# Second block's mixers: GpSimd's products and weight splits moved to VectorE and ScalarE up to the output projection

## The chip, the cores and the metric

One core of a Trainium2 chip runs the whole program in one launch. Its engines are TensorE (PE in the rows; PEld is its weight load), VectorE (DVE), ScalarE (ACT), GpSimd (POOL) and SyncE (SP), which issues the weight loads. The metric is the device time of one execution in microseconds (us); lower is better.

## The reference, cut to what matters

A first block (a chunked mLSTM and a sparse attention side by side, then a mixture of 32 experts) is followed by a second block of two layers over 272 tokens (16 meta tokens and 256 of the sequence) of width 1024. The change lies in the mixers of the second block. Cut down, a layer there is:

```
proj = rms_norm(h, norm_mix_g[l]) @ w_in[l]
q, k, v, xr, gate = jnp.split(proj, splits, axis=-1)
q = apply_partial_rope(rms_norm(q, q_norm_g[l]), cos, sin)      # k alike
o_attn = rms_norm(diff_attention(q, k, v, lam), subln_g[l]) * (1.0 - lam_init)
xc = causal conv of xr, width 4;  r, i = sigmoid(xc @ w_rg + b_rg), sigmoid(xc @ w_ig + b_ig)
log_a = 8 * r * log_sigmoid(lru_L);  a = exp(log_a)
u = sqrt(max(-expm1(2 * log_a), 0)) * i * xc                    # factor 1 at t = 0
h_t = a_t * h_(t-1) + u_t
o_rec = rms_norm(h_t * gelu(gate), rec_norm_g[l])
h = h + concat(o_attn, o_rec) @ w_out[l]
h = h + (silu(g) * u) @ w_down[l],   g, u = rms_norm(h, norm_ffn_g[l]) @ w_gu[l]
```

All of it is float32.

## The kernel before, in words

**Products in three parts.** Weights stream from HBM in tiles of 128x4096. `run` walks a list of items; a weight item is a 128x1024 piece (128x512 for `w_out`), and LEAD = 4 items ahead of its use `split` (line 1446) turns it into a high half `wh` (a cast to fp32r, ScalarE, L1449) and a low half `wl = w - wh` (L1452 on VectorE, or L1454 when an engine was named, which before the change is GpSimd for some pieces). `wh` and `wl` each have a ring of LEAD + 1 = 5 buffers. An input-projection item is 24 matmuls, three for each of 8 pieces of the contraction (L339: high x high, L340: high x low activations, L341: low weights), 128x272 each, into one bank of PSUM.

**The items of a mixer** (`layer2`), in their order: X, four pieces for the recurrent input with its convolution (`conv`); four pieces of k and four of q (`qkin`), among them the steps `lru1` to `lru5` of the recurrence; then G, four pieces of the gate, and V, four pieces of v, among them `qk_norm`, the per-head steps `knorm`, `scores`, `mix`, `turn`, `value`, `oc`, `orow`, and the recurrent branch's `gelu1`, `gelu2`, `rec_sq`, `rec_c`, `rec_r`; then R, the eight pieces of the output projection on the recurrent half, and eight on the attention half.

**q and k.** For each piece ScalarE copies the product out as `z` (L1775) and squares it (L1777), VectorE multiplies it by the cosines (L1778), TensorE rotates `z` (L1790), VectorE multiplies by the sines (L1791) and adds (L1792). `z` has a ring of two buffers (tag `vin`): the third piece's `z` waits for the first piece's L1792. TensorE gathers the sums of squares in `ps_qs` (L1787). `qk_norm` then makes all reciprocal roots in one chain of small VectorE steps (L1800, L1802, three rounds of L211 to L213, and L1804), 128x48 each. TensorE broadcasts the result (`ps_rqb`, L1811, in `knorm`), which stands on its queue behind the gate's second piece G[1] and before the third.

**The recurrence.** On tiles of 128x1088: ScalarE takes logarithms and exponentials in `lru1`; VectorE does L1708 and L1709, GpSimd squares (L1711) in `lru2`; VectorE does L1715 and L1716, GpSimd two products (L1717, L1718) in `lru3`; VectorE L1723 and L1725, GpSimd a product (L1724) in `lru4`; VectorE four scans in `lru5` (L1729). In `gelu1` GpSimd does the last product (L1740). In `rec_r` VectorE scales (L1762), ScalarE makes the high halves `yhi`, GpSimd the low halves `ylo` (L1454), which the items R read.

**Order.** The lists are written out by hand, but each engine's queue is set by the framework's scheduler from them, and each engine runs its queue strictly in order. Small chains that others wait for are marked `high_priority`. `split` without a named engine puts `wl` behind `self.mark`, the last step of the last reciprocal root traced so far:

```
if eng is None and self.mark is not None:
    with self.tc.issue_after(self.mark):
        nc.vector.tensor_tensor(lo, src, hi.bitcast(F32), op=ALU.subtract)
```

Of the kernel before, what the change touches and what calls it, by code (L numbers as in the profile page):

```python
# [13 lines left out]
AF = mybir.ActivationFunctionType  # L14
ALU = mybir.AluOpType
# [179 lines left out]
class Kernel:  # L195
# [1429 lines left out]
    def layer2(self, l):  # L1625

        tc, nc, d = self.tc, self.nc, self.d
# [6 lines left out]
        def tile_(nm, shape, dt=F32, tag=None, bufs=1):  # L1634
            return B["px"].tile(shape, dt, name=f"{nm}_{l}", tag=tag or nm, bufs=bufs)

        def part(nm, k):

            key = (nm, k // 4)
            if key not in B:  # L1640
                tag = {("yhi", 0): "rr", ("yhi", 1): "ii", ("ylo", 0): "xc", ("ylo", 1): "gl"}[key]
                B[key] = tile_(f"{nm}{k // 4}", [P, 4, T2], F32R, tag)
            return B[key][:, k % 4]
# [61 lines left out]
        def lru2():  # L1705
            th, c, y, t = B["rr"], B["xc"], B["ry"], B["rt"]

            nc.vector.scalar_tensor_tensor(t, th, 1.0, c, op0=ALU.add, op1=ALU.mult)  # L1708
            nc.vector.scalar_tensor_tensor(c, t, 2.0, c, op0=ALU.subtract, op1=ALU.mult)  # L1709

            nc.gpsimd.tensor_tensor(t, y, y, op=ALU.mult)  # L1711

        def lru3():
            th, c, y, t, ii = B["rr"], B["xc"], B["ry"], B["rt"], B["ii"]
            nc.vector.scalar_tensor_tensor(t, t, -0.5, th, op0=ALU.mult, op1=ALU.mult)  # L1715
            nc.vector.scalar_tensor_tensor(y, t, 1.5, y, op0=ALU.add, op1=ALU.mult)  # L1716
            nc.gpsimd.tensor_tensor(ii, ii, c, op=ALU.mult)  # L1717
            nc.gpsimd.tensor_tensor(y, y, th, op=ALU.mult)  # L1718

        def lru4():  # L1720
            th, c, y, t, ii = B["rr"], B["xc"], B["ry"], B["rt"], B["ii"]

            nc.vector.tensor_scalar(y[:, :, 0:1], th[:, :, 0:1], 0.5, 0.5, op0=ALU.mult, op1=ALU.add)  # L1723
            nc.gpsimd.tensor_tensor(ii, ii, y, op=ALU.mult)  # L1724
            nc.vector.tensor_scalar(t, c, -2.0, -1.0, op0=ALU.mult, op1=ALU.add)  # L1725

        def lru5():
# [3 lines left out]
        def gate(n):  # L1731
            def f(po):
                nc.vector.tensor_tensor(B["gl"][:, n], po, self.rb, op=ALU.mult)
            return f

        def gelu1():
            gl, t = B["gl"], B["rt"]
            nc.scalar.activation(t, gl, AF.Square)
            nc.vector.tensor_scalar(t, t, 0.044715, 1.0, op0=ALU.mult, op1=ALU.add)
            nc.gpsimd.tensor_tensor(t, t, gl, op=ALU.mult)  # L1740

        def gelu2():
            gl, t, hr = B["gl"], B["rt"], B["ry"]
# [14 lines left out]
        def rec_r():  # L1758
            hr = B["ry"]
            r = self.col_rows(B["recr"], T2, f"rec{l}")  # L1760
            for n in range(4):
                nc.vector.scalar_tensor_tensor(hr[:, n], hr[:, n], self.col("recg", 4 * l + n), r,  # L1762
                                               op0=ALU.mult, op1=ALU.mult)
                self.split(part("yhi", 4 + n), part("ylo", 4 + n), hr[:, n], nc.gpsimd)


        def qkin(i):
# [38 lines left out]
        def knorm(i):  # L1806
            def f():
                prb = self.ps(f"ps_rqb{l}{i}")
                for j, (o, m) in enumerate(self.chunks(T2)):
                    for c in range(2):  # L1810
                        nc.tensor.matmul(prb[64 * c : 64 * c + 64, o : o + m],  # L1811
                                         B["rq"][:m, j, 2 * i + c : 2 * i + c + 1].to_broadcast([m, 64]),
                                         self.ident[:m, :m], start=True, stop=True)
                nc.vector.tensor_tensor(B["qk"][:, i], B["qk"][:, i], prb[:, :T2], op=ALU.mult)
            return f


        def vin(n):
            def f(po):
                v = tile_(f"v{n}", [P, T2], tag="vin", bufs=2)  # L1820
                nc.vector.tensor_tensor(v, po, self.rb, op=ALU.mult)
                B["v", n] = v
            return f
# [51 lines left out]
        def mix(h):  # L1875
            def f():
                e, ea, sm = B["e", h], B["ea", h], B["sm", h]
                parts = [(e, P, slice(0, T2), 0), (e, P, slice(T2, 416), 1)]
                parts += [(ea, 16, slice(0, 16), 2)] if l == 0 else []
                for ap, m, cs, q in parts:  # L1880
                    nc.vector.reciprocal(sm[:m, q], sm[:m, q])
                    nc.vector.tensor_tensor(sm[:m, q, 1:2], sm[:m, q, 1:2], self.nlam[:m, l : l + 1], op=ALU.mult)
                    nc.vector.tensor_scalar(ap[:m, 0, cs], ap[:m, 0, cs], sm[:m, q, 0:1], None, op0=ALU.mult)
                    nc.vector.scalar_tensor_tensor(ap[:m, 0, cs], ap[:m, 1, cs], sm[:m, q, 1:2], ap[:m, 0, cs],
                                                   op0=ALU.mult, op1=ALU.add)
            return f
# [33 lines left out]
        def oc(h):  # L1920
            def f():
                B["or", h] = self.col_sums(B["px"], B["osq", h][:, t0:], nq, P, f"ro{l}{h}")
            return f
# [55 lines left out]
        pool = nc.gpsimd  # L1979
# [5 lines left out]
        def inp(c, n, then, eng=None):  # L1985
            return self.lin_f(("win", l, c), n * 1024, KT, xin, self.after_rows(then), eng)[0]
# [11 lines left out]
        def out(k, part, last):  # L1998
            a = slice(4 * part, 4 * part + 4)
            return self.lin_f(("wout", l, k // 4), (k % 4) * 1024 + 512 * part, 4, lambda: tuple(x[a] for x in xmid(a)),  # L2000
                              add_mix(k, last), pool if last else None)[0]

        R = [out(k, 1, False) for k in range(KT)]
        G = [inp(1, n, gate(n), pool if n > 1 else None) for n in range(4)]
        V = [inp(4, n, vin(n), pool) for n in range(4)]
        it += [G[0], qk_norm, G[1], knorm(4), knorm(5), G[2], scores(0), knorm(6), G[3], scores(1),
               mix(0), knorm(7), gelu1, V[0], turn(0), scores(2), vtr(0), mix(1), gelu2,
               V[1], value(0), turn(1), scores(3), vtr(1), mix(2), rec_sq, V[2], oc(0), value(1), turn(2), vtr(2), mix(3), rec_c,
               V[3], orow(0), oc(1), value(2), turn(3), vtr(3), rec_r, R[0], orow(1), oc(2), value(3), R[1], R[2],
               orow(2), oc(3), R[3], R[4], orow(3)]  # L2010
        it += R[5:]
# [31 lines left out]
```

## Time and profile before

| what | value |
|---|---|
| median of 3 runs | 1934.74 us (1932.25 to 1937.94) |
| the profiled execution's own time | 1937.82 us |
| its span, first to last instruction | 1936.1 us |
| granted TensorE clock, mean over the span | 0.935 |
| busy share: PE, DVE, ACT, POOL | 90%, 42%, 29%, 14% |
| layer 0's mixer / layer 1's mixer (us from the start) | about 1190 to 1370 / 1585 to 1735 |

The profile's busy shares are averages over the whole program. The change touches two stretches of some 130 us, one in each layer, and is read from the rows of those: the busy time of each engine in slices, what TensorE waited for there, and the instructions in order of time with their durations. A row of an instruction gives its time from start to end; neighbours on VectorE overlap a little, so that from one start to the next is about 0.08 us less. The granted clock tells which of its two levels TensorE ran at: 1.00 is 2.4 GHz, 0.50 is 1.2 GHz.

### The profile page before, as it was taken

What the parts mean: (1) busy time and instruction counts of PE and PEld (TensorE: products, weight loads), DVE (VectorE), ACT (ScalarE), POOL (GpSimd) and SP (SyncE); (2) the same over time, 40 slices, a digit from 0 to 9 for tenths busy, and PEclk for the clock granted to TensorE, in tenths of its full rate; (3) what the DMA queues carried; (4) which work ended last, traced back from release to release, by engine and by line L of the source; (5) the groups of instructions that cost most, each with busy time, mean ns of one, the idle gap of its engine ahead of it and who ended that gap; (6) DMA issues with size and microseconds to landing.
All of it is one profiled execution on the core that took longest, in us unless ns stands there. A gap on an engine that the chain in (4) does not pass through costs nothing.

```text
span 1936.1 us, 34266 instructions
## 1 busy us (share of the span) xinstructions
PE 1739.4 (90%) x14551; PEld 1231.3 (64%) x14552; DVE 810.0 (42%) x1806; ACT 568.3 (29%) x1127; POOL 264.4 (14%) x259
## 2 busy tenths in 40 slices
PE   6999899866999997799999766989999998889998
PEld 3786743433544543454354334977999998789998
DVE  3573632211122222122222114587666557876653
ACT  2564511100111110011010102525544445354442
POOL 2322300000000000000000001051233103223320
PEclk8999889976999998899999878888999999889999
DMA  9658589999899999999999997220443453125441
GB/s 387 236 183 322 203 351 427 428 428 425 367 428 429 426 426 427 428 425 428 428 426 427 426 428 330 88 88 1 174 174 134 167 206 120 56 95 192 166 152 51
DMA packets 42698, 556.68 MB, mean 288 GB/s; under 512 B 4788, under 2 KB 5964, under 8 KB 8360
## 3 DMA queue, kind: packets, MB, share of 16 engines
q1 hardware_dynamic: 40368, 548.41, 69.4%
q0 software_dynamic: 1200, 4.29, 0.6%
q8 instruction: 116, 1.90, 0.4%
q10 hardware_dynamic: 968, 1.70, 0.3%
q14 instruction: 46, 0.38, 0.1%
HBM read 553.32 MB, written 1.06 MB: 286 GB/s over the span
## 4 chain that ended last, share of the span: by engine, by line
PE 56%; DMA 12%; DVE 5%; ACT 1%; issue 0%; ACTq 0%; POOL 0%; DVEq 0%; POOLq 0%
DMA we<-wexp 12%; PE ps_lin L339 9%; PE ps_lin L340 9%; PE ps_lin L341 9%; PE ps_l L1320 7%; PE ps_u L1320 6%; PE ps_d L1320 6%; PE ps_g L1286 2%; PE ps_c L1383 2%; DVE qk L1792 1%; PE ps_at L1363 1%; PE ps_rqb L1811 0%; PE ps_ri L1686 0%; PE ps_pg L1348 0%; PE nm0ss L1500 0%
## 5 line engine op out<-in xcount | busy, mean ns | idle before, releaser
L339 PE MATMUL ps_lin<-xhi,wh 128*128 128x272 f32 (+1 forms) x1024 | 301.6, 295 | 0.2 <-ACT xhi L1430 0.2
L340 PE MATMUL ps_lin<-xlo,wh 128*128 128x272 f32 (+1 forms) x1024 | 297.3, 291 | 1.0 <-DVE xlo L1431 1.0
L341 PE MATMUL ps_lin<-xhi,wl 128*128 128x272 f32 (+1 forms) x1024 | 297.4, 291 | 0.0
L1320 PE MATMUL ps_d<-we,at 128*32 128x256 f32 (+1 forms) x2048 | 223.0, 482 | 48.5 <-DMA we<-wexp 39.0
L1320 PE MATMUL ps_l<-we,xg 128*32 128x256 f32 (+1 forms) x2048 | 217.2, 461 | 29.7 <-DMA we<-wexp 29.5
L1320 PE MATMUL ps_u<-we,xg 128*32 128x256 f32 (+1 forms) x2048 | 212.4, 454 | 25.5 <-DMA we<-wexp 24.6
L339 PEld LDWEIGHTS ps_lin<-xhi,wh 128*128 128x128 f32 x1024 | 197.4, 193 | 2.8 <-DVE qk L1778 0.8
L340 PEld LDWEIGHTS ps_lin<-xlo,wh 128*128 128x128 f32 x1024 | 197.3, 193 | 1.8 <-DVE xlo L1431 1.4
L341 PEld LDWEIGHTS ps_lin<-xhi,wl 128*128 128x128 f32 x1024 | 197.3, 193 | 0.0
L1320 PEld LDWEIGHTS ps_d<-we,at 128*32 128x32 f32 (+1 forms) x2048 | 90.4, 128 | 165.0 <-issue 102.2
L1320 PEld LDWEIGHTS ps_l<-we,xg 128*32 128x32 f32 (+1 forms) x2048 | 88.6, 123 | 139.4 <-issue 97.2
L1320 PEld LDWEIGHTS ps_u<-we,xg 128*32 128x32 f32 (+1 forms) x2048 | 87.1, 121 | 128.0 <-issue 76.1
L1387 DVE TENSOR_TENSOR hT<-hT,ps_c 128x512 f32<-128x512 f32 x128 | 79.4, 681 | 151.7 <-PE ps_c L1383 151.7
L1406 POOL TENSOR_TENSOR hT<-hT,g 128x1024 f32<-128x1024 f32 x1 | 3.3, 3261 | 946.1 <-DVE ssm L1404 946.1
L1449 ACT CAST wh<-wgu 128x1024 fp32r<-128x1024 f32 x88 | 92.2, 1049 | 122.1 <-PE ps_lin L340 121.4
L1452 DVE TENSOR_TENSOR wl<-wgu,wh 128x1024 fp32r<-128x1024 f32 x88 | 108.2, 1231 | 41.6 <-ACT wh L1449 41.6
L1332 DVE TENSOR_SCALAR gl<-ps_u 128x512 f32<-128x512 f32 (+1 forms) x36 | 20.3, 572 | 217.1 <-PE ps_u L1324 217.1
L1364 ACT COPY at<-ps_at 128x512 f32<-128x512 f32 (+1 forms) x36 | 17.3, 492 | 299.9 <-PE ps_at L1363 299.1
L339 PE MATMUL ps_lin<-ahi,wh 128*128 128x272 f32 (+1 forms) x352 | 100.6, 286 | 0.0
L341 PE MATMUL ps_lin<-ahi,wl 128*128 128x272 f32 (+1 forms) x352 | 100.0, 284 | 0.0
L340 PE MATMUL ps_lin<-alo,wh 128*128 128x272 f32 (+1 forms) x352 | 99.9, 284 | 0.0
L1288 ACT ACTIVATE xg<-ps_g,modc,a2c 128x128 f32<-128x128 f32 (+1 forms) x120 | 43.8, 452 | 171.0 <-PE ps_g L1286 171.0
(677 smaller groups left out, 2920.9 us busy)
## 6 DMA issues: line engine op xcount, KB each, us to landing
we<-wexp SPq DMA_DIRECT2D x192, 2048.0 KB, 27.3
wgu<-wgu SPq DMA_DIRECT2D x22, 2048.0 KB, 7.7
win<-win SPq DMA_DIRECT2D x14, 2048.0 KB, 9.1
wada<-wada SPq DMA_DIRECT2D x12, 2048.0 KB, 7.9
wdn<-wdn SPq DMA_DIRECT2D x16, 1408.0 KB, 6.0
wout<-wout SPq DMA_DIRECT2D x6, 2048.0 KB, 7.7
wint<-wint SPq DMA_DIRECT2D x2, 2048.0 KB, 9.3
wins<-wins SPq DMA_DIRECT2D x1, 1264.0 KB, 28.1
```

The lines of the kernel that those rows point to most:

```text
L339: nc.tensor.matmul(po[:m, :nn], hi[:, a], xh[k], start=(k == 0), stop=False)
L340: nc.tensor.matmul(po[:m, :nn], hi[:, a], xl[k], start=False, stop=False)
L341: nc.tensor.matmul(po[:m, :nn], lo[:, a], xh[k], start=False, stop=(k == nk - 1))
L1286: nc.tensor.matmul(p, self.x[:, tt, k * P : k * P + P], oh[:, tt], start=(tt == 0), stop=(tt == 1))
L1288: nc.scalar.activation(xg[:, k], pg[:, (k - k0) * n : (k - k0) * n + n], AF.Identity, scale=self.a2c[:, k : k + 1], bias=self.modc2[:, k : ...
L1320: nc.tensor.matmul(dst[b][s], lhs(k, b), ws[k // 4][:, o : o + wd], start=(k == 0 and b % per == 0), stop=False)
L1332: nc.vector.tensor_scalar(gl[i], pu[i], 7.0, 0.5, op0=ALU.min, op1=ALU.mult)
L1363: nc.tensor.transpose(pt[:, c * P : c * P + P], li[i][:, c * P : c * P + P], self.ident)
L1383: nc.tensor.matmul(pc[s][:, (tt - t0) * wd : (tt - t0) * wd + wd], gt[b][rows[s], tt * P : tt * P + P], y[b // per][rows[s], (b % per) * w ...
L1387: nc.vector.tensor_tensor(a, a, pc[s].rearrange("p (a b) -> p a b", a=per), op=ALU.add)
L1449: nc.scalar.copy(hi, src)
L1452: nc.vector.tensor_tensor(lo, src, hi.bitcast(F32), op=ALU.subtract)
```

## The change

In each of the two layers, five products of 128x1088 leave GpSimd: the square L1711 goes to ScalarE (an activation), and L1717, L1718, L1724 and L1740 go to VectorE. So do the low halves `wl` of six weight pieces (G[2], G[3] and V[0] to V[3]) and the four low halves `ylo` of the recurrent branch. GpSimd keeps the low halves of the output projection's last eight pieces and its work in the feed-forward part.

```diff
--- before.py
+++ after.py
@@ -1708,20 +1708,20 @@
             nc.vector.scalar_tensor_tensor(t, th, 1.0, c, op0=ALU.add, op1=ALU.mult)
             nc.vector.scalar_tensor_tensor(c, t, 2.0, c, op0=ALU.subtract, op1=ALU.mult)
 
-            nc.gpsimd.tensor_tensor(t, y, y, op=ALU.mult)
+            nc.scalar.activation(t, y, AF.Square)
 
         def lru3():
             th, c, y, t, ii = B["rr"], B["xc"], B["ry"], B["rt"], B["ii"]
             nc.vector.scalar_tensor_tensor(t, t, -0.5, th, op0=ALU.mult, op1=ALU.mult)
             nc.vector.scalar_tensor_tensor(y, t, 1.5, y, op0=ALU.add, op1=ALU.mult)
-            nc.gpsimd.tensor_tensor(ii, ii, c, op=ALU.mult)
-            nc.gpsimd.tensor_tensor(y, y, th, op=ALU.mult)
+            nc.vector.tensor_tensor(ii, ii, c, op=ALU.mult)
+            nc.vector.tensor_tensor(y, y, th, op=ALU.mult)
 
         def lru4():
             th, c, y, t, ii = B["rr"], B["xc"], B["ry"], B["rt"], B["ii"]
 
             nc.vector.tensor_scalar(y[:, :, 0:1], th[:, :, 0:1], 0.5, 0.5, op0=ALU.mult, op1=ALU.add)
-            nc.gpsimd.tensor_tensor(ii, ii, y, op=ALU.mult)
+            nc.vector.tensor_tensor(ii, ii, y, op=ALU.mult)
             nc.vector.tensor_scalar(t, c, -2.0, -1.0, op0=ALU.mult, op1=ALU.add)
 
         def lru5():
@@ -1737,7 +1737,7 @@
             gl, t = B["gl"], B["rt"]
             nc.scalar.activation(t, gl, AF.Square)
             nc.vector.tensor_scalar(t, t, 0.044715, 1.0, op0=ALU.mult, op1=ALU.add)
-            nc.gpsimd.tensor_tensor(t, t, gl, op=ALU.mult)
+            nc.vector.tensor_tensor(t, t, gl, op=ALU.mult)
 
         def gelu2():
             gl, t, hr = B["gl"], B["rt"], B["ry"]
@@ -1761,7 +1761,7 @@
             for n in range(4):
                 nc.vector.scalar_tensor_tensor(hr[:, n], hr[:, n], self.col("recg", 4 * l + n), r,
                                                op0=ALU.mult, op1=ALU.mult)
-                self.split(part("yhi", 4 + n), part("ylo", 4 + n), hr[:, n], nc.gpsimd)
+                self.split(part("yhi", 4 + n), part("ylo", 4 + n), hr[:, n], nc.vector)
 
 
         def qkin(i):
@@ -2001,8 +2001,8 @@
                               add_mix(k, last), pool if last else None)[0]
 
         R = [out(k, 1, False) for k in range(KT)]
-        G = [inp(1, n, gate(n), pool if n > 1 else None) for n in range(4)]
-        V = [inp(4, n, vin(n), pool) for n in range(4)]
+        G = [inp(1, n, gate(n)) for n in range(4)]
+        V = [inp(4, n, vin(n)) for n in range(4)]
         it += [G[0], qk_norm, G[1], knorm(4), knorm(5), G[2], scores(0), knorm(6), G[3], scores(1),
                mix(0), knorm(7), gelu1, V[0], turn(0), scores(2), vtr(0), mix(1), gelu2,
                V[1], value(0), turn(1), scores(3), vtr(1), mix(2), rec_sq, V[2], oc(0), value(1), turn(2), vtr(2), mix(3), rec_c,
```

The scheduler places the moved work anew. On VectorE's queue in layer 0, from the sines of the first q piece on (`qk` and `z` belong to q and k, `ii`, `rt`, `ry`, `rr`, `xc` to the recurrence, `wl` are low halves of weights; the numbers tell buffers apart), this stood before:

```order
L1791 TENSOR_TENSOR z_0_11391<-ps_rot_11443,sin 128x272
L1778 SCALAR_TENSOR_TENSOR qk_0_10955<-ps_lin_11410,qgs,cos 128x272
L1792 TENSOR_TENSOR qk_0_10955<-qk_0_10955,z_0_11391 128x272
L1715 SCALAR_TENSOR_TENSOR rt_10952<-rt_10952,rr_11235 128x1088
L1716 SCALAR_TENSOR_TENSOR ry_10951<-rt_10952,ry_10951 128x1088
L1791 TENSOR_TENSOR z_0_11435<-ps_rot_11488,sin 128x272
L1725 TENSOR_SCALAR rt_10952<-xc_10953 128x1088
L1792 TENSOR_TENSOR qk_0_10955<-qk_0_10955,z_0_11435 128x272
L1778 SCALAR_TENSOR_TENSOR qk_0_10955<-ps_lin_11455,qgs,cos 128x272
L1791 TENSOR_TENSOR z_0_11480<-ps_rot_11532,sin 128x272
```

and this stands there now:

```order
L1717 TENSOR_TENSOR ii_11236<-ii_11236,xc_10953 128x1088
L1791 TENSOR_TENSOR z_0_11391<-ps_rot_11443,sin 128x272
L1715 SCALAR_TENSOR_TENSOR rt_10952<-rt_10952,rr_11235 128x1088
L1452 TENSOR_TENSOR wl_11452<-win_01_10795,wh_11451 128x1024
L1778 SCALAR_TENSOR_TENSOR qk_0_10955<-ps_lin_11410,qgs,cos 128x272
L1792 TENSOR_TENSOR qk_0_10955<-qk_0_10955,z_0_11391 128x272
L1716 SCALAR_TENSOR_TENSOR ry_10951<-rt_10952,ry_10951 128x1088
L1791 TENSOR_TENSOR z_0_11435<-ps_rot_11488,sin 128x272
L1452 TENSOR_TENSOR wl_11496<-win_01_10795,wh_11495 128x1024
L1778 SCALAR_TENSOR_TENSOR qk_0_10955<-ps_lin_11455,qgs,cos 128x272
L1718 TENSOR_TENSOR ry_10951<-ry_10951,rr_11235 128x1088
L1725 TENSOR_SCALAR rt_10952<-xc_10953 128x1088
```

The products L1717 and L1718 and two weight splits have come in between the steps of q, k and the recurrence. Further on in the same queue, the end of `qk_norm`'s chain was:

```order
L211 TENSOR_TENSOR rq_t<-rq_y 128x48
L1733 TENSOR_TENSOR gl_10954<-ps_lin_11597,rb_10895 128x272
L212 SCALAR_TENSOR_TENSOR rq_t<-rq_t,rqv_11577 128x48
L213 SCALAR_TENSOR_TENSOR rq_y<-rq_t,rq_y 128x48
L1804 TENSOR_TENSOR rq_y<-rq_y,nm0r_y 128x48
L1729 SCALAR_TENSOR_TENSOR ry_10951<-rt_10952,ii_11236 128x272 x4
```

and is now:

```order
L211 TENSOR_TENSOR rq_t<-rq_y 128x48
L212 SCALAR_TENSOR_TENSOR rq_t<-rq_t,rqv_11577 128x48
L213 SCALAR_TENSOR_TENSOR rq_y<-rq_t,rq_y 128x48
L1452 TENSOR_TENSOR wl_11594<-win_04_10797,wh_11593 128x1024
L1452 TENSOR_TENSOR wl_11640<-win_04_10797,wh_11639 128x1024
L1804 TENSOR_TENSOR rq_y<-rq_y,nm0r_y 128x48
L1814 TENSOR_TENSOR qk_0_10955<-qk_0_10955,ps_rqb_11623 128x272
```

The two weight splits, whose place is behind the marked root, stand right before the chain's last step L1804 (L1733 and the scans L1729 are no longer here). The head of that chain was:

```order
L1800 SCALAR_TENSOR_TENSOR rqv_11577<-ps_qs_11186,r_0_11187 128x48
L1802 TENSOR_SCALAR rqv_11577<-rqv_11577 128x48
L209 TENSOR_SCALAR rq_y<-rqv_11577 128x48
L211 TENSOR_TENSOR rq_t<-rq_y 128x48
L212 SCALAR_TENSOR_TENSOR rq_t<-rq_t,rqv_11577 128x48
```

and is now:

```order
L1800 SCALAR_TENSOR_TENSOR rqv_11577<-ps_qs_11186,r_0_11187 128x48
L1729 SCALAR_TENSOR_TENSOR ry_10951<-rt_10952,ii_11236 128x272 x4
L1733 TENSOR_TENSOR gl_10954<-ps_lin_11597,rb_10895 128x272
L1802 TENSOR_SCALAR rqv_11577<-rqv_11577 128x48
L209 TENSOR_SCALAR rq_y<-rqv_11577 128x48
```

The four scans of the recurrence, which stood behind L1804, now stand inside the chain, behind its first step, with the gate's product L1733. GpSimd's queue has none of the moved products and splits any more, and layer 1's queues change in the same way.

## Rows read from the trace of the kernel before

**Rows 1.** Stretches: length, busy us of PE, PEld, DVE, ACT, POOL, PEclk, DMA

```profile
1260.00:1280.00 20.00, 15.91 (x101) 15.30 (x101) 19.86 (x16) 4.47 (x7) 18.78 (x8) 0.85 0.29 106
1640.00:1660.00 20.00, 9.78 (x58) 8.58 (x58) 19.43 (x30) 2.75 (x4) 13.07 (x6) 0.73 0.30 106
```

**Rows 2.** Who waited for whom, layer 0's mixer, TensorE: total us, times, longest

```profile
PE ps_rqb L1811 <- DVE rq_y L1804: 5.4, 1, 5.4
PE ps_rot L1790 <- ACT z L1775: 5.4, 3, 4.1
```

**Rows 3.** Layer 0, VectorE in order of time: start, us, operation, [idle before]

```profile
1254.63 1.29 DVE L1708 SCALAR_TENSOR_TENSOR rt<-rr,xc 128x1088 f32<-128x1088 f32 x1 [1.49 <-ACT xc L1702]
...
1257.39 1.22 DVE L1452 TENSOR_TENSOR wl<-win,wh 128x1024 fp32r<-128x1024 f32 x1
1258.53 0.49 DVE L1778 SCALAR_TENSOR_TENSOR qk<-ps_lin,qgs,cos 128x272 f32<-128x272 f32 x1
1258.94 0.43 DVE L1791 TENSOR_TENSOR z<-ps_rot,sin 128x272 f32<-128x272 f32 x1
...
1260.69 3.60 DVE L1715 SCALAR_TENSOR_TENSOR rt<-rt,rr 128x1088 f32<-128x1088 f32 x1
1264.33 3.36 DVE L1716 SCALAR_TENSOR_TENSOR ry<-rt,ry 128x1088 f32<-128x1088 f32 x1
...
1267.96 2.55 DVE L1725 TENSOR_SCALAR rt<-xc 128x1088 f32<-128x1088 f32 x1
1270.44 2.71 DVE L1792 TENSOR_TENSOR qk<-qk,z 128x272 f32<-128x272 f32 x1
...
1281.70 0.19 DVE L209 TENSOR_SCALAR rq_y<-rqv 128x48 int32<-128x48 int32 x1
1281.93 0.21 DVE L211 TENSOR_TENSOR rq_t<-rq_y 128x48 f32<-128x48 f32 x1
...
1286.47 0.21 DVE L1804 TENSOR_TENSOR rq_y<-rq_y,nm0r_y 128x48 f32<-128x48 f32 x1
1286.60 2.56 DVE L1729 TENSOR_TENSOR_SCAN ry<-rt,ii 128x272 f32<-128x272 f32 x4
```

**Rows 4.** Order of time, layer 0, GpSimd

```profile
1260.44 2.71 POOL L1717 TENSOR_TENSOR ii<-ii,xc 128x1088 f32<-128x1088 f32 x1
1263.09 6.84 POOL L1454 TENSOR_TENSOR wl<-win,wh 128x1024 fp32r<-128x1024 f32 x2
1269.89 2.96 POOL L1718 TENSOR_TENSOR ry<-ry,rr 128x1088 f32<-128x1088 f32 x1
```

**Rows 5.** Order of time, layer 0, VectorE: two shapes with GpSimd idle

```profile
1246.09 0.72 DVE L1698 TENSOR_SCALAR rr<-rr 128x1088 f32<-128x1088 f32 x1
...
1249.73 0.44 DVE L1792 TENSOR_TENSOR qk<-qk,z 128x272 f32<-128x272 f32 x1
```

**Rows 6.** Order of time, layer 0, ScalarE: a cast behind G[1]; a square of 128x1088

```profile
1281.23 1.04 ACT L1449 CAST wh<-win 128x1024 fp32r<-128x1024 f32 x1 [6.28 <-PE ps_lin L340]
...
1301.92 1.10 ACT L1738 ACTIVATE rt<-gl 128x1088 f32<-128x1088 f32 x1
```

**Rows 7.** Who waited for whom, layer 1's mixer, TensorE

```profile
PE ps_rqb L1811 <- DVE rq_y L1804: 6.1, 1, 6.1
...
PE ps_v L1829 <- DVE v L1821: 1.4, 1, 1.4
PE ps_pt L1893 <- DVE e L1884: 1.2, 1, 1.2
```

**Rows 8.** Order of time, layer 1, VectorE: a 128x4 step of scores

```profile
1674.57 2.31 DVE L1863 SCALAR_TENSOR_TENSOR mx<-mx,rq_y 128x4 f32<-128x4 f32 x1
```

**Rows 9.** Order of time, layer 1, GpSimd: the gelu product

```profile
1674.39 2.48 POOL L1740 TENSOR_TENSOR rt<-rt,gl 128x1088 f32<-128x1088 f32 x1 [6.38 <-DVE rt L1739]
```

**Rows 10.** Busy time in the stretch behind turn(1)'s wait in layer 1

```profile
1683.80:1686.50 2.70, 2.70 (x13) 1.72 (x12) 2.31 (x6) 2.70 (x9) 0.00 (x0) 0.50 0.00 0
```

## The prediction

> **What bounds the kernel now.** I read four views, each of the two mixers alone. The busy times in stretches come first: from 1260 to 1280 us VectorE was busy for 19.86 of 20 us and GpSimd for 18.78, while TensorE had 4 us with nothing to do; layer 1 shows the same from 1640 to 1660, with TensorE busy for only 9.78 [rows 1]. The waits say for what TensorE stood still: 5.4 us in layer 0 and 6.1 us in layer 1 for the last step of `qk_norm`'s chain, L1804 [rows 2, 7], and up to 4.1 us for a `z` of q [rows 2], in a row that reads the same for layer 1; that `z` itself waits for an L1792 of VectorE, whose buffer it takes. So VectorE sets the time here; the order of time shows what it is busy with. The wide L1715 took 3.60 us and L1716 3.36 us, where L1708, the same operation on the same shape, took 1.29 us [rows 3]. L1725 took 2.55 us and its like 0.72; an L1792 took 2.71 us and another 0.44 [rows 3, 5]. The long ones have their ends in common with GpSimd: L1715 ends at 1264.29 us, one plain duration after GpSimd's L1717 (1263.15); L1725 ends 0.58 us after the second split (1269.93), the L1792 0.30 us after L1718 (1272.85) [rows 3, 4]. L1791, which reads PSUM, kept its 0.43 us. I read this as standing still: a VectorE instruction with its inputs in SBUF lets the GpSimd instruction in front of it finish, and the wait is counted as busy.
>
> The Trainium skill has this as a rule: "SBUF — State Buffer", section "SBUF: two separate sides", calls the port pair that the two engines share an exclusive lock, held for the whole instruction. The rows above agree.
>
> **The change, part by part.** *The chain up to L1804, layer 0.* In the new order VectorE has the following from the start of L1708 (1254.63) to the start of L1804, priced from start to start without GpSimd [rows 3, 5]: seven wide two-input products (L1708, L1709, L1715, L1716, and the moved L1717, L1718, L1724) at 1.21 us, 8.5; six weight splits (five of them moved) at 1.14, 6.8; four L1778 at 0.41, 1.6; four L1791, five L1792 and two L1733 at 0.35, 3.9; L1725 at 0.64; L1723 at about 0.1; four scans, which now stand inside the chain, 2.5; twelve small steps of the chain at 0.23, 2.8. The sum is 26.8 us. Before, the same stretch took 1286.47 - 1254.63 = 31.8 us, of which the like sum without the moved work and the scans is 15.0, so that 16.8 us was standing still. Removed: 16.8; added: 5.7 of splits, 3.6 of products, 2.5 of scans, 11.8 together. L1804 comes 5.0 us sooner; I take 4.8, with 0.2 for hand-overs between engines that the prices do not hold. The bounds are 0, if all of it were eaten by new waits, and 16.8, if nothing that was added stood on the path; the order puts it there, so I stay by the sum.
>
> Does anything else hold VectorE up on the way? The second of the two splits in front of L1804 needs a cast by ScalarE, which needs a buffer that TensorE frees with the end of G[1]; before, that was at 1281.23 us, and the cast took 1.04 [rows 6]. The `z` of the last q piece may now start behind an L1792 that by the prices above ends near 1269 us and not at 1273.15 [rows 3], so that TensorE's 4.1 us wait goes and G[1] ends by 1277.2; the cast is done by 1278.3, and VectorE, by the prices, comes to that split at 1280. Nothing holds it up. TensorE then waits for L1804 in one piece, at least 4 us and more if G[1] keeps the full clock. Behind a wait of 1.2 us already the clock stood at 0.50 [rows 7, 10]; it stands so behind this one, before and after, and I count no difference.
>
> *Layer 1's chain* is the same list and has the same stalls: another 4.8. Two layers: 9.6 us.
>
> *The square on ScalarE* takes about 1.0 us (its like took 1.10 [rows 6]) and delays the next `z` by that; two wide products, a split and more stand on VectorE's queue in front of that `z`'s sines, so I cost it at nothing. Without that cover it would be 1.0 us a layer.
>
> *The attention part.* VectorE gets V[3]'s split (1.14) and the gelu product L1740 (1.20) and loses GpSimd's lock: in layer 1 a step of 128x4 took 2.31 us, ending with GpSimd's L1740 [rows 8, 9], and TensorE waited for what stood behind it, 1.4 us for L1821 and 1.2 us for `e` in turn(1); then it ran 2.7 us at clock 0.50, which costs half of that [rows 7, 10]. That is 2.6 + 1.3 = 3.9 us to be had. Going down the new queue with the same prices, turn(0) is late by 0.4, turn(1) by 0.2 and turn(2) by 0.7; I keep 2.6 us. In layer 0 TensorE had no such wait; the new queue brings `e` some 0.1 to 0.7 us before TensorE comes to it, with nothing to spare, and I take 0.6 as loss. Bounds for both layers: a gain of 3.9, a loss in the second rival below.
>
> *The four `ylo`* cost VectorE 1.4 us (four at 0.35) and put the next head's root behind them; on the other side TensorE gets each sooner than from GpSimd, and the lock goes here too. I cost the exchange at 0, between +1.4 and -1.4 us a layer.
>
> *What stays:* the output projection's splits on GpSimd and their locks, the feed-forward, the first block; no DMA is issued otherwise.
>
> Sum: 9.6 + 2.6 - 0.6 = 11.6 us. The profiled execution took 1937.8 us, so it would take 1926.2; it lies 3.1 us above the median of the three runs shown, 1934.7, and against that median the time is **1923.1 us**.
>
> **The rivals.** *First, G[1] is late.* If the `z` of the last q piece still starts as late as before, TensorE ends G[1] at 1281.2 as it did; the cast (1.04) and the second split (1.14) follow, and L1804 starts at 1283.4, a gain of 3.0 us a layer. With the attention part at nothing that is 6 us: 1929. For it: VectorE's queue has no slack. Against: L1792 stands before, not behind, the splits that matter.
>
> *Second, and slower: VectorE becomes late for every head.* TensorE ran through layer 0's attention part without a wait, so each delay of `mix` or `scores` on the fuller queue is a new wait. One like turn(1)'s, 1.2 us, with the 1.3 us that the low clock took behind it [rows 7, 10], costs 2.5 us. At all eight turns of the two layers that is 20 us against the chains' 9.6: 1945. It decides from four of the eight turns on. For it: nothing to spare in my walk down the queue. Against: the lock in that part, 2.3 us in layer 1, is as long as the two instructions that take its place.
>
> *Third, the long rows are VectorE's own work.* Then nothing is given back and 11.8 us a layer is added: 1958. The rows with a plain twin speak against it. The Trainium skill, "Perfetto Trace Analysis", section "Optimizing Scalar/DVE Operations", says that moving work off a saturated VectorE, to GpSimd even, may make sense, and this change goes the other way; the same section warns that the two share a port. The rows bear out the warning, and I give the rule 3 in 100.
>
> *Fourth, more than the sum:* the chains give all of 5.0, layer 1's attention part its 3.9 with no loss in layer 0, and the `ylo` 1.4 a layer: 16.7 us, 1918.
>
> **How the numbers follow.** The forecast has 0.70, the first rival 0.13, the fourth 0.08, the second 0.06, the third 0.03. The range takes in the fourth and the first with 1 us of scatter of the median: 1916.5 to 1930.5. A measurement of this kernel can tell 0.3%, 5.8 us, from no change. The forecast, the fourth and 0.05 of the first rival lie beyond that: 0.83 faster; the other 0.08 of the first and half of the second make 0.11 the same; the rest, 0.06, is slower.
>
> **What would show it.** Right: VectorE's L1715, L1716 and L1792 at 1.3 and 0.44 us; L1804 some 27 us after L1708's start instead of 32; one wait for it of 4 to 8 us and none for `z` above 1 us; no wait at L1829 in layer 1. Wrong: long rows with GpSimd idle; the same 5 us wait for L1804 as before; waits at turn(0) to turn(3) of over 1 us with a clock of 0.50 behind them.

## The result and the profile after

The change takes 1913.9 us (median of 4, 1907.5 to 1916.6) against 1934.95 us before: 0.989 of the time, 95% interval 0.9876 to 0.9905. The gain is 21.1 us where 11.6 were forecast, and 1913.9 lies below the range.

Busy times in stretches at the same distance behind L1708 as in [rows 1] (same columns). GpSimd is at 0 in both, TensorE's idle time fell from 10.2 to 7.4 us in layer 1's stretch, and rose from 4.1 to 6.0 in layer 0's, into which most of the wait for L1804 now falls. VectorE is as full as before in layer 0 but has 7 us free in layer 1.

```profile
1252.31:1272.31 20.00, 14.02 (x107) 13.40 (x106) 19.65 (x41) 5.92 (x10) 0.00 (x0) 0.93 0.29 106
1624.85:1644.85 20.00, 12.63 (x94) 11.24 (x96) 12.88 (x32) 3.18 (x4) 0.00 (x0) 0.74 0.17 71
```

The order of time on VectorE, layer 0, answers to [rows 3, 5]:

```profile
1246.94 1.29 DVE L1708 SCALAR_TENSOR_TENSOR rt<-rr,xc 128x1088 f32<-128x1088 f32 x1 [1.49 <-ACT xc L1702]
...
1252.80 1.29 DVE L1715 SCALAR_TENSOR_TENSOR rt<-rt,rr 128x1088 f32<-128x1088 f32 x1
1254.00 1.22 DVE L1452 TENSOR_TENSOR wl<-win,wh 128x1024 fp32r<-128x1024 f32 x1
1255.13 0.50 DVE L1778 SCALAR_TENSOR_TENSOR qk<-ps_lin,qgs,cos 128x272 f32<-128x272 f32 x1
1255.54 0.43 DVE L1792 TENSOR_TENSOR qk<-qk,z 128x272 f32<-128x272 f32 x1
1255.89 1.29 DVE L1716 SCALAR_TENSOR_TENSOR ry<-rt,ry 128x1088 f32<-128x1088 f32 x1
...
1258.99 1.29 DVE L1718 TENSOR_TENSOR ry<-ry,rr 128x1088 f32<-128x1088 f32 x1
1260.19 0.72 DVE L1725 TENSOR_SCALAR rt<-xc 128x1088 f32<-128x1088 f32 x1
...
1271.17 2.35 DVE L1452 TENSOR_TENSOR wl<-win,wh 128x1024 fp32r<-128x1024 f32 x2
1273.44 0.20 DVE L1804 TENSOR_TENSOR rq_y<-rq_y,nm0r_y 128x48 f32<-128x48 f32 x1
```

L1715 and L1716 take 1.29 us (3.60 and 3.36 before), L1725 0.72 (2.55), L1792 0.44 (2.71). L1804 starts 26.50 us behind L1708; before it was 31.84. The two splits of 1271.17 stand in front of it, as the order said. ScalarE's square, and its cast behind G[1], which answers to [rows 6]:

```profile
1249.88 1.12 ACT L1711 ACTIVATE rt<-ry 128x1088 f32<-128x1088 f32 x1 [0.37 <-DVE xc L1709]
...
1266.24 1.04 ACT L1449 CAST wh<-win 128x1024 fp32r<-128x1024 f32 x1 [3.17 <-PE ps_lin L340]
```

What TensorE waited for in layer 0 (total us, times, longest), for [rows 2]:

```profile
PE ps_rqb L1811 <- DVE rq_y L1804: 7.4, 1, 7.4
PE ro03r L1476 <- DVE ro_y L213: 1.9, 1, 1.9
PE ps_rot L1790 <- ACT z L1775: 1.3, 2, 0.7
PE ps_lin L339 <- ACT yhi L1449: 1.0, 1, 1.0
PE ps_lin L340 <- DVE ylo L1454: 0.9, 1, 0.9
```

There is one wait for L1804, of 7.4 us, and none of 4 us for `z`; the sum of the two fell from 10.8 to 8.7 us. Layer 1 has the same rows, with 2.2 at the fourth root and 0.8 at `ylo`. The waits of [rows 7] at L1829 and turn(1) are gone; two short ones are new, the first at turn(2), the second at turn(0):

```profile
PE ps_pt L1893 <- DVE mx L1863: 0.4, 1, 0.4
PE ps_pt L1893 <- DVE e L1884: 0.3, 1, 0.3
```

Between marks that every trace has, the starts of TensorE's rows give the table below. "x" is the first `ps_x` of layer 0's mixer, "q" the first `ps_rqb` (L1811) of a layer, "y" its first matmul on `yhi`, "r" the broadcast of its fourth head's root (`ro03r`, `ro13r`). The traces are of before (its second one is e5, with idle memsets far behind) and of the change (the last is e6, likewise).

| stretch | before | change | forecast gain |
|---|---|---|---|
| start to x | 1196.6, 1198.1, 1191.0 | 1188.8, 1197.2, 1195.1, 1193.2 | 0 |
| x to q, layer 0 | 90.2, 89.7, 90.1 | 84.9, 84.9, 84.5, 84.8 | 4.8 |
| q to y, layer 0 | 49.4, 49.3, 49.4 | 46.6, 46.6, 46.4, 46.6 | -0.6 |
| y to r, layer 0 | 19.2, 18.8, 19.1 | 19.8, 19.9, 15.6, 15.6 | 0 |
| r to q, layer 1 | 301.7, 301.7, 301.7 | 296.4, 296.5, 296.5, 296.5 | 4.8 |
| q to y, layer 1 | 44.5, 44.4, 43.4 | 40.8, 40.8, 41.1, 41.2 | 2.6 |
| y to r, layer 1 | 18.0, 18.0, 18.0 | 18.5, 18.5, 17.0, 17.0 | 0 |
| x to last r | 523.0, 521.9, 521.8 | 507.0, 507.2, 501.0, 501.7 | 11.6 |

The chains gave 5.2 us each and layer 1's attention part 3.1. The rest was not forecast: 2.8 us in layer 0's attention part, and a stretch behind `yhi` that takes 15.6 or 19.8 us in executions of the same kernel. The mixers as a whole gain 15 or 21 us by that. The first of the four traces of the change also had the shortest first block of all 14 traces (1188.8 us, others to 1198.1), so the pair that I read first put 7.7 us into code that the change does not touch.

### The profile page after: what moved, and what is told of

It is laid out like the page before. It is cut to its first block, busy times and chain, and to the rows that moved or that the text cites. A ratio compares the mean times of both kernels' runs of the same rounds, so it can differ in the third digit from the quotient of the medians.

```text
span 1912.6 us, 34255 instructions
## 1 busy us (share of the span) xinstructions
PE 1722.9 (90%) x14551; PEld 1221.2 (64%) x14552; DVE 794.9 (42%) x1834; ACT 570.6 (30%) x1129; POOL 197.6 (10%) x229
## 4 chain that ended last, share of the span: by engine, by line
PE 57%; DMA 12%; DVE 5%; ACT 1%; issue 0%; ACTq 0%; DVEq 0%
DMA we<-wexp 12%; PE ps_lin L339 9%; PE ps_lin L340 9%; PE ps_lin L341 9%; PE ps_l L1320 7%; PE ps_u L1320 6%; PE ps_d L1320 6%; PE ps_g L1286 2%; PE ps_c L1383 2%; DVE wl L1452 1%; PE ps_at L1363 1%; PE ps_rqb L1811 0%; PE ps_ri L1686 0%; PE ps_pg L1348 0%; PE nm0ss L1500 0%
## 5 line engine op out<-in xcount | busy, mean ns | idle before, releaser
L1320 PE MATMUL ps_d<-we,at 128*32 128x256 f32 (+1 forms) x2048 | 215.4, 465 | 46.8 <-DMA we<-wexp 36.9
L1320 PE MATMUL ps_u<-we,xg 128*32 128x256 f32 (+1 forms) x2048 | 217.5, 466 | 31.5 <-DMA we<-wexp 31.5
L1364 ACT COPY at<-ps_at 128x512 f32<-128x512 f32 (+1 forms) x36 | 17.3, 492 | 302.4 <-PE ps_at L1363 301.6
```

Of the source, the lines that this page charges most:

```text
L1320: nc.tensor.matmul(dst[b][s], lhs(k, b), ws[k // 4][:, o : o + wd], start=(k == 0 and b % per == 0), stop=False)
```

## The experiments

All times are medians beside runs of before on the same chip (1933.2 to 1934.7 us), but for e9 and e10, which are one execution each; "mixers" is the last row of the table, and a "fall" is a stretch in which TensorE's granted clock is at 0.50.

**e1, e9 and e10: the change and before once more.** No edit.

> The changed kernel once more. Measured so far: 21.1 us less by the medians, 23.5 us by the two profiled spans, of which 7.7 us lie ahead of the first ps_x of layer 0's mixer (1196.6 us before, 1188.8 after), where no instruction was changed, and 16.0 us between that point and the fourth root row of layer 1's mixer (523.0 us before, 507.0 after). Theory A, the first block scatters from run to run: the mixers take 507.0 us again within 0.5, the first ps_x comes anywhere from 1187 to 1197 us, and the medians differ by 14 to 21 us. Rival B, the change makes the first block faster too (its program lies differently in memory): first ps_x at 1189 us again within 1.5, and the medians differ by 20 us or more.

Measured: 1912.5 us, 0.9877 of before (0.9861 to 0.9894). First `ps_x` at 1197.2, mixers 507.2: rival B falls, the first block scatters. But then the medians should differ by less than the 22.2 us they do; theory A's 507.0 cannot be the usual value either.

> The changed kernel, one more trace. Two of its traces have TensorE at clock 0.50 for 10.2 us behind the 1.0 us wait for yhi in both layers (mixers 507.0 and 507.2 us); the trace with the 24 memsets behind them has the same instructions and the same waits there and no low clock in layer 0, 6.8 us in layer 1 (mixers 501.7). Theory: whether the clock falls there is drawn anew in each execution, so this trace may have either, the mixers anywhere from 500 to 507.2 us, with L1804 26.5 us behind L1708 and the waits the same in any case; the first ps_x from 1188 to 1198. Rival: it is the program that decides: 507.1 us again within 0.3.

Measured: 1913.0 us, mixers 501.0, 6.2 us less than in e1, in the same kernel. The rival falls. The two traces have the same waits at `yhi` and `ylo`, TensorE's order of time in e1,

```profile
1328.75 0.39 PE L339 MATMUL ps_lin<-yhi,wh 128*128 128x272 f32 x1 [1.04 <-ACT yhi L1449]
1330.02 0.59 PE L340 MATMUL ps_lin<-ylo,wh 128*128 128x272 f32 x1 [0.88 <-DVE ylo L1454]
```

and in e9:

```profile
1326.03 0.39 PE L339 MATMUL ps_lin<-yhi,wh 128*128 128x272 f32 x1 [1.04 <-ACT yhi L1449]
1327.30 0.40 PE L340 MATMUL ps_lin<-ylo,wh 128*128 128x272 f32 x1 [0.88 <-DVE ylo L1454]
```

The second matmul takes 0.59 us in the one and 0.40 in the other. The stretches of 10.2 us from 0.55 us behind the start of `yhi`'s first matmul (columns as in [rows 1], the granted clock third from the end), e1:

```profile
1329.30:1339.50 10.20, 9.48 (x35) 8.32 (x36) 4.85 (x20) 2.39 (x6) 0.00 (x0) 0.50 0.00 0
```

and e9:

```profile
1326.58:1336.78 10.20, 9.48 (x68) 8.75 (x69) 7.84 (x29) 4.05 (x9) 0.00 (x0) 1.00 0.01 2
```

TensorE ran at 1.2 GHz in the one, behind this wait, and stayed at 2.4 GHz in the other; there it did about twice as many matmuls. The two executions ran on different chips, so the chip could be the cause. But behind x an execution takes 725.5 us in e1 and 717.9 in e9 (its time less its start to x). Four of e1's five executions took 1911.0 to 1913.2 us; with e1's figure they would have had x at 1185.5 to 1187.7 us, sooner than in any of the 14 traces, with e9's at 1193.1 to 1195.3. By this estimate most executions on e1's chip had no such fall either, or a shorter one.

The Trainium skill, "TensorE: Matmul & The Clock Gate", section "What's actually happening", says that the number of slow matmuls at a kernel's start varies between runs of one kernel. The two traces show the like for a fall in mid-kernel (35 matmuls in 10.2 us and 68).

> The kernel before, one more trace. Its two traces so far (one with the memsets at the end) have the low clock behind the 0.6 us wait for ro00r in layer 0, 13.7 and 10.2 us of it before and behind the yhi wait, and the mixers at 523.0 and 521.9 us. Theory: with a wait of 0.6 us ahead of yhi's 1.0 us the fall is there each time: 8 us or more of low clock in that place, mixers 521 to 524 us. Rival: the fall is as much a matter of chance as in the changed kernel: none or 3.4 us of it, mixers 516 to 519 us.

Measured: 1929.5 us, 13.7 us of low clock in that place again, mixers 521.8. The rival falls. In before the fall comes earlier, behind a wait of 0.6 us that I had not counted. TensorE's order of time there in its first trace, and the stretches before the fall, from it to `yhi`'s wait, and from `yhi`'s first matmul on:

```profile
1328.64 1.03 PE L1476 MATMUL ro00r<-ident,ro_y 128*128 128x128 f32 x6 [0.60 <-DVE ro_y L213]
1329.60 0.83 PE L1467 MATMUL ro01c<-ones,osq 128*128 128x1 f32 x6
...
1336.15 0.59 PE L339 MATMUL ps_lin<-yhi,wh 128*128 128x272 f32 x1 [1.04 <-ACT yhi L1449]
```

```profile
1328.10:1332.00 3.90, 3.36 (x20) 2.79 (x21) 3.23 (x15) 0.92 (x3) 0.00 (x0) 0.99 0.00 0
1332.00:1335.11 3.11, 3.11 (x15) 2.26 (x13) 1.01 (x5) 1.48 (x4) 0.00 (x0) 0.50 0.00 0
1336.15:1345.70 9.55, 9.23 (x32) 7.69 (x33) 4.67 (x18) 2.38 (x6) 3.44 (x4) 0.51 0.00 0
```

Behind the wait came the root's broadcast and six sums of one column (128x1); from 1332.0 us the clock is at 0.50, and it is still there when the `yhi` item begins, so that its matmuls run at half speed. All three traces of before show 10.2 to 13.7 us of low clock here.

**e2, e3 and e4: the parts of the change.**

```
e2   G[2], G[3], V[0..3]: inp(...) without pool; all else as before
e3   L1711 nc.scalar.activation(..., Square); L1717, L1718, L1724 nc.vector; all else as before
e4   e2 and e3 together; L1740 and ylo (L1764) stay nc.gpsimd
```

> Only the six weight splits a layer move; the recurrence's square and products, the gelu product and the ylo stay on GpSimd. From the start of L1708 to the start of L1804 it took 31.8 us before and 26.5 us after. Theory: VectorE stands still for each GpSimd instruction that it meets, 2.5 to 3 us for each of three or four products, and no longer 3.4 us for each of four to five splits, but has five splits of 1.14 us more: 31.8 - 14 + 5.7 + some 2.5 of scans = 26 to 28 us, and the whole run 8 to 13 us below before. Rival: the stall depends on the products alone (they write what VectorE reads next): then L1804 comes later than before, 36 us or more, and the run is slower than before by 8 us.

> Only the recurrence's square and three products move (L1711 to ScalarE; L1717, L1718, L1724 to VectorE); the splits, the gelu product and the ylo stay on GpSimd. Theory: the splits on GpSimd go on stopping VectorE, some 10 to 14 us before L1804, the products' stalls of 7 to 8 us go and 3.6 us of products come: 31.8 - 7.5 + 3.6 = 27 to 29 us from L1708 to L1804, and the run 4 to 10 us below before. Rival: splits and products stop VectorE only where both engines want the same tiles: then this takes all of the gain at L1804 (26.5 us) and the run is as fast as the change.

Measured: e2 0.9956 (0.994 to 0.9971), 1927.1 us, from L1708 to L1804 29.8 us; e3 0.9975 (0.9964 to 0.9986), 1930.75 us, 30.5 us in layer 0 and 29.8 in layer 1. Both rivals fall: either kind of GpSimd work stops VectorE, whether or not the tiles are shared. But the theory's size was off too: 26 to 28 and 27 to 29 us were expected to L1804, and the runs gained 7.6 and 4.0 us where 8 to 13 and 4 to 10 were expected. At L1804 in layer 0 the two halves gain 2.1 and 1.4 us, both together 5.3. The rows tell why. VectorE in e2, then GpSimd:

```profile
1258.98 2.26 DVE L1452 TENSOR_TENSOR wl<-win,wh 128x1024 fp32r<-128x1024 f32 x1
...
1261.58 2.34 DVE L1792 TENSOR_TENSOR qk<-qk,z 128x272 f32<-128x272 f32 x1
1263.85 1.28 DVE L1715 SCALAR_TENSOR_TENSOR rt<-rt,rr 128x1088 f32<-128x1088 f32 x1
...
1268.26 2.29 DVE L1725 TENSOR_SCALAR rt<-xc 128x1088 f32<-128x1088 f32 x1
```

```profile
1260.13 3.49 POOL L1717 TENSOR_TENSOR ii<-ii,xc 128x1088 f32<-128x1088 f32 x1
1266.53 3.44 POOL L1718 TENSOR_TENSOR ry<-ry,rr 128x1088 f32<-128x1088 f32 x1 [2.91 <-DVE ry L1716]
```

VectorE in e3, then GpSimd:

```profile
1261.28 3.13 DVE L1715 SCALAR_TENSOR_TENSOR rt<-rt,rr 128x1088 f32<-128x1088 f32 x1
...
1264.74 2.21 DVE L1792 TENSOR_TENSOR qk<-qk,z 128x272 f32<-128x272 f32 x1
...
1270.04 2.91 DVE L1725 TENSOR_SCALAR rt<-xc 128x1088 f32<-128x1088 f32 x1
```

```profile
1260.49 6.17 POOL L1454 TENSOR_TENSOR wl<-win,wh 128x1024 fp32r<-128x1024 f32 x2 [38.76 <-ACT wh L1449]
1268.83 3.52 POOL L1454 TENSOR_TENSOR wl<-win,wh 128x1024 fp32r<-128x1024 f32 x1 [2.18 <-ACT wh L1449]
```

In e2 a moved split takes 2.26 us and L1792 2.34 beside products that now take 3.49 and 3.44 us (2.71 and 2.96 in [rows 4]); in e3 L1715 takes 3.13 and L1725 2.91. What is left on GpSimd meets a fuller VectorE queue, and each stops the other.

> The change without its late part: the gelu product L1740 and the four ylo stay on GpSimd. Past L1804 the change gained 2.8 us in layer 0 and 3.6 us in layer 1 up to the first yhi matmul. Theory A, the clock: TensorE fell to its low level twice around the chain (behind the wait for z and behind that for L1804) and falls once now; so layer 0 keeps its 2.8 us here, and layer 1 loses at most the 2.6 us of its two waits with 1.3 us of low clock behind them: the run is 0 to 4 us slower than the change. Rival B, the lifted lock in the attention part itself: both gains go, and the run is 6 us or more slower than the change, with the same L1804.

Measured: 1917.1 us, 0.9911 (0.9893 to 0.9928), 4.6 us above e1; L1804 at 26.5; layer 0's q to y 46.7 as in the change, layer 1's 41.8, 0.8 us more. Theory A allowed 4 us at most and is missed by 0.6. Rival B falls: the gelu product and the `ylo` are not what gave layer 0 its 2.8 us. Who did: the wait for `ro00r` of 0.6 us is in all traces of before and in e3, and in none of e2, e4 and the change, and layer 0's q to y is 49.3 to 49.5 in the first group and 46.4 to 46.7 in the second. With the splits on VectorE, the last step of that root (L213) no longer stands behind an L1821 on its queue that waits for TensorE. VectorE in before,

```profile
1328.07 0.44 DVE L1821 TENSOR_TENSOR v<-ps_lin,rb 128x272 f32<-128x272 f32 x1 [0.26 <-PE ps_lin L341]
1328.43 0.15 DVE L213 SCALAR_TENSOR_TENSOR ro_y<-ro_t,ro_y 128x3 f32<-128x3 f32 x1
```

and in e2:

```profile
1324.27 0.16 DVE L213 SCALAR_TENSOR_TENSOR ro_y<-ro_t,ro_y 128x3 f32<-128x3 f32 x1
1325.04 0.44 DVE L1821 TENSOR_TENSOR v<-ps_lin,rb 128x272 f32<-128x272 f32 x1 [0.61 <-PE ps_lin L341]
```

So the 2.8 us came with the splits; the wait went with the new order of the queue, not with the lock.

**e5 and e6: 24 idle memsets.**

```
+ [nc.gpsimd.memset(pad, 0.0) for 24 tiles of 128x1]     # layer 1, start of the feed-forward part
```

> The kernel before with 24 tiny GpSimd memsets (128x1) at the start of layer 1's feed-forward part, behind all that is in question; every instruction ahead of that is the same, in the same order. What is open: the change is 20 to 22 us faster by the medians, its mixers by 16.0 us in both traces; the rest lies in the first block, where no instruction differs. With what follows the first ps_x taken from the traces, the executions of the kernel before had their first ps_x at 1190 to 1198 us (middle 1193.5, 21 executions), those of the change at 1182 to 1191 and once 1197 (middle 1187, 9 executions), those of the three part-changes at 1190 to 1200 (middle 1195 to 1197). Theory A: each program has its own first block of some 6 us to either side, whatever was changed, by how it lies in memory or starts: then this program's middle may be anywhere from 1186 to 1198, and 24 instructions at the end can move it by over 2 us. Rival B: it belongs to what the change moves: then the middle is 1193.5 within 1.5, the median 1934.7 within 2.

> The changed kernel with the same 24 memsets at the start of layer 1's feed-forward part. Theory A, the 6 us of the first block are the program's own draw: the middle of the first ps_x may move from 1187 to any place up to 1198, and the median with it, up to 1924. Rival B, they belong to what the change moves: middle at 1187 within 1.5, median 1912 to 1915. Both: the mixers take 507.0 us.

Measured: e5 1935.2 us, 1.0009 (0.9997 to 1.0021), first `ps_x` 1198.1; e6 1913.9 us, first `ps_x` 1193.2. The figures of rival B for the medians hold, yet its reason does not: the first block of e6 is as long as others', and its mixers took 501.7 us, not the 507.0 on which both sides were agreed. The "middle of 1187 us" was worked out with 507 us for every execution and fell with it.

**e7: L1804 ahead of the two splits.**

```
- nc.vector.tensor_tensor(B["rq"], B["rq"], r("r1"), op=ALU.mult)
+ self.mark = nc.vector.tensor_tensor(B["rq"], B["rq"], r("r1"), op=ALU.mult).ins
```

> The changed kernel, with the mark set at L1804, the chain's last step, so that the two weight splits of V[0] and V[1], which stood between the last root and L1804, follow L1804. Theory, the place on the queue decides and each split costs its 1.14 to 1.2 us there: from L1708 to L1804 24.1 us instead of 26.5, TensorE's wait for L1804 5.0 us instead of 7.4, the mixers 2.4 us less a layer, 502 us. Rival: the wait moves to the next step (L1814 and the scores behind the two splits), and the mixers stay at 506 to 507 us.

Measured: 1908.7 us, 0.9861 (0.9837 to 0.9886). L1804 comes 24.35 us behind L1708, TensorE's wait is 5.2 us, in both layers. VectorE:

```profile
1279.79 0.21 DVE L213 SCALAR_TENSOR_TENSOR rq_y<-rq_t,rq_y 128x48 f32<-128x48 f32 x1
1280.03 0.21 DVE L1804 TENSOR_TENSOR rq_y<-rq_y,nm0r_y 128x48 f32<-128x48 f32 x1
1280.15 2.35 DVE L1452 TENSOR_TENSOR wl<-win,wh 128x1024 fp32r<-128x1024 f32 x2
```

The place on the queue decides; the rival falls. The mixers took 494.1 us, 7 less than the change without a fall behind `yhi` in layer 0 (the theory had 4.8): 2.1 and 2.2 us in the two stretches up to q (2.4 each in the theory), and 3.1 from y to r in layer 1, where this trace has no fall either.

**e8 and e12: the recurrent half sooner.**

```
- V[3], orow(0), oc(1), value(2), turn(3), vtr(3), rec_r, R[0],
+ V[3], rec_r, orow(0), oc(1), value(2), turn(3), vtr(3), R[0],     (e12: and the mark of e7)
```

> The changed kernel, with rec_r (the scaling L1762, yhi and ylo) moved in the list of items from behind vtr(3) to just behind V[3], so that yhi and ylo are made some 8 us ahead of the item R[0] that reads them. In the change TensorE waits 1.0 us for yhi and 0.8 to 0.9 us for ylo in each layer and then runs 10.2 us at clock 0.50. Theory, the clock falls behind this wait: without it go 1.9 us of waiting and up to 5.1 us of the low clock, 4 to 7 us a layer, the mixers 493 to 499 us. Rival, the clock falls for what TensorE did before (the small matmuls of the attention part): only the 1.9 us go, mixers 503 us, with the low clock at the same place; or the wait comes back at rec0r, for the root that is now asked for sooner, and nothing is won.

> The changed kernel with the mark at L1804 and with rec_r just behind V[3]. Each alone: mixers 494.1 us (mark; no fall at yhi in that trace) and 498.5 us (rec_r; no wait for yhi, but new ones, 1.0 to 1.2 us for rec0r and rec1r). Theory, the two add: 2.2 us a layer from the mark on 498.5, 494 us, and the fall at yhi is excluded and not drawn, so that the time scatters with the first block alone: 1902 to 1907. Rival: the new waits for the root cost what the yhi wait cost, and the time is that of the mark alone, 1908.7 within 2.

Measured: e8 1912.1 us (0.9895, 0.9873 to 0.9918), mixers 498.5: the waits for `yhi` and `ylo` and the fall behind them are gone, but TensorE waits 1.0 to 1.2 us for `rec0r` and `rec1r` and 2.0 for `ro11r`. The mixers are within the theory, yet the median is within 2 us of that of the change on the same chip (e6, with the memsets, 1913.9). e12 1912.95 us (0.9892, 0.9872 to 0.9912), mixers 504.2, with the clock at 0.50 behind the new waits of 1.2 (`rec0r`) and 1.9 us (`ro01r`) in layer 0: no faster than e7 alone. The theory falls in e12, and so does its rival (1908.7 within 2); a wait was moved, not removed. In e12 the clock fell behind the new wait for `rec0r`; in e8's trace the same wait of 1.2 us had no fall behind it.

**e11: the last GpSimd work too.**

```
- add_mix(k, last), pool if last else None)[0]
+ add_mix(k, last))[0]                                       (and the mark of e7)
```

> The changed kernel with the mark at L1804 and with the last work of GpSimd in the mixer, the eight splits of the output projection's attention half, on VectorE too. In the change two steps of the last root chain (L211 and L213, 128x3) take 1.1 to 1.3 us instead of 0.16 where these splits run, and TensorE waits 1.9 to 2.2 us for ro03r and ro13r with 3.4 us of clock 0.50 behind it. Theory, the lock: the steps take 0.16 us, the waits fall below 0.5 us and the fall behind them goes: 3 to 4 us a layer, the mixers 486 to 490 us against 494.1 with the mark alone, the time 1900 to 1904. Rival: the wait is the length of the root chain itself (eleven steps with their hand-overs), and eight splits of 0.65 us on the busier VectorE make it longer: the same 2 us or more, mixers 494 to 498.

Measured: 1902.0 us (1899.5 to 1907.6), 0.984 (0.9823 to 0.9858), as expected, but mixers 492.2 for 486 to 490. Two steps of the fourth head's root in e7, beside GpSimd's splits,

```profile
1339.15 1.13 DVE L211 TENSOR_TENSOR ro_t<-ro_y 128x3 f32<-128x3 f32 x1
...
1340.51 1.26 DVE L213 SCALAR_TENSOR_TENSOR ro_y<-ro_t,ro_y 128x3 f32<-128x3 f32 x1
```

and the same lines in e11:

```profile
1337.08 0.16 DVE L211 TENSOR_TENSOR ro_t<-ro_y 128x3 f32<-128x3 f32 x1
...
1337.47 0.16 DVE L213 SCALAR_TENSOR_TENSOR ro_y<-ro_t,ro_y 128x3 f32<-128x3 f32 x1
```

The lock was the cause of the wait in layer 0 (2.0 us to none); in layer 1 0.9 us of 2.2 stay. This version beats both kernels: 32.5 us below before.

## Why the prediction was wrong in size

**Right: the lock and the chain.** The long rows were standing still; all four operations went to the plain prices, and 26.5 us from L1708 to L1804 stand against a sum of 26.8 and 0.2 for hand-overs. The chains gave 10.4 us for 9.6. The rule of the Trainium skill in "SBUF — State Buffer", section "SBUF: two separate sides", is borne out by e2 and e3, where the lock stays with whatever GpSimd keeps (L1725 at 2.29 and 2.91 us), and e11, where it goes (0.16 us).

**Right: layer 1's attention part.** 2.6 us were forecast, 3.1 came. The waits at L1829 and turn(1) are gone; turn(0) is late by 0.3 us and turn(2) by 0.4, where 0.4 and 0.7 were expected. The low clock of [rows 10] is itself not in every trace of before: e10 has the same two waits without it, and takes 43.4 us from q to y and not 44.4. L1740 and V[3]'s split cost nothing that shows.

**Wrong: the clock.** The step that failed is "In layer 0 TensorE had no such wait", with 0.6 us of loss taken there, together with "I count no difference": the sum put the low clock at nothing in layer 0's attention part and behind `yhi`. I priced each wait by its own length, read those above 1 us, and took the clock into account at one place of layer 1. Without a fall behind `yhi` in layer 0 the mixers' gain is 20.9 us (522.2, the mean of before, less 501.35), 9.3 more than the sum. Of these some 3.5 lie in layer 0's attention part, some 4.5 behind `yhi` in the two layers, and the other 1.3 in terms that were right.

In layer 0's attention part, q to y, 0.6 us of the gain are the wait for `ro00r`. The rest is the clock. TensorE was busy at 0.50 there in two stretches before, behind q and behind `ro00r` (columns as in [rows 1]):

```profile
1286.73:1294.40 7.67, 7.67 (x45) 6.93 (x46) 3.19 (x6) 0.00 (x0) 0.00 (x0) 0.50 0.00 0
1331.95:1335.11 3.16, 3.16 (x15) 2.31 (x13) 1.01 (x5) 1.51 (x4) 0.00 (x0) 0.50 0.00 0
```

and in one after, since the longer wait for L1804 takes up more of the 10.2 us of low clock:

```profile
1273.70:1279.90 6.20, 6.20 (x39) 5.47 (x40) 0.88 (x2) 0.00 (x0) 0.00 (x0) 0.50 0.00 0
```

By the matmuls of e1 and e9 above, a microsecond at 1.2 GHz costs about half of one while TensorE is busy. The 4.6 us less are then worth 2.3 us, with the wait 2.9, by this estimate; 2.8 were measured. Reckoned so, q to y without its waits and without that half is 42.4 to 42.5 us in all seven traces of the table. It holds for y to r too: TensorE was busy at 0.50 for 6.8 to 9.1 us in before and for 9.5 us or none in the change, and what is left is 12.2 to 12.7 us in all seven. Not every low stretch costs: the 6.8 us that before had behind the wait for `z` lie ahead of L1804, where VectorE's chain sets the time, and that stretch gained what the chain gave.

That the 0.6 us wait brings on the fall is read from traces with it (the three of before and e3) and without it (the change, e2, e4); it was not changed by itself. Why the clock falls behind the wait for `yhi` in some executions and not in others stays open. With the fall the mixers gain 15.1 us, without it 20.9; the medians, 19.2 to 22.2 us below before, lie near the second.

**Wrong: the width.** The range allowed 1 us of scatter of the median, and had no term for a fall that comes in some executions only. The medians agree within 2 us (1933.2 to 1935.0 in before, 1912.5 to 1913.9 in the change with e1 and e6), but single executions don't. Of one kernel the first block alone varied from 1191.0 to 1197 us in before and from 1188.8 to 1197.2 in the change, and the mixers of the change by 6 us. How much of the medians' 21 us is mixers and how much a draw of first blocks can't be told to better than some 2 us from these traces.

**The rivals.** G[1] was not late: ScalarE's cast came at 1266.24 us, VectorE to the two splits at 1271.17. VectorE did not become late for the heads: the new waits are 0.3 and 0.4 us. The third rival is ruled out by the order of time: L1715 and L1716 take 1.29 us with GpSimd at 0. The fourth was nearest, 16.7 us, but by terms that don't account for what came. What the four `ylo` cost or gave, forecast at nothing, is not settled: e4, with them on GpSimd, had 17.3 us from y to r in layer 0, between the two values of the change, and its own 3.4 us of low clock there. The waits say that little is at stake: TensorE's first wait for `ylo` is 0.9 and 0.8 us in the change (layers 0 and 1) and 0.5 in e4, and the 0.9 us for `ro11r` that e4 has in layer 1 is gone in the change.

## What to carry to other kernels

Where two engines stop each other, half a move gains less than half (2.1 and 1.4 us against 5.3 here): what stays behind goes on locking. A half was still worth something (7.6 and 4.0 us of run time, against 22.2 for the whole), but its gain can't be read off the whole. Price a wait of TensorE with the low clock that follows it, unless another engine sets the time of that stretch, and look for short ones too: 10 to 17 us at half speed followed one of 0.6 us in all four traces that have it. Read more than one trace of each kernel before giving a difference of a few us a cause.

## What was not expected

The same instructions with the same waits (1.04 and 0.88 us) were followed by 10.2 us at clock 0.50 in two traces of the changed kernel and by none in two others (one of them with the memsets). And a stretch that no change touches, the first 1190 us, scattered by 9 us over 14 traces, more than half of what the change is worth by its forecast.
